# A diffusion trunk step on one core: modulation's column tiles over six stages, other operand places and product order in the w2 groups

## The chip, the core and the metric

The kernel runs on one NeuronCore of a Trainium2 chip. TensorE (PE in the profile; PEld is its weight load) multiplies matrices, VectorE (DVE) and ScalarE (ACT) work on elements, GpSimd (POOL) does almost nothing here, and SyncE (SP) issues the transfers, nearly all on one queue. The metric is the device time of one execution in microseconds. Single runs of this kernel took 1923.6, 1925.41 and 1929.54 us; the median is 1925.41 us.

## The reference, cut to what matters

One layer of a hybrid trunk over 512 latent and 128 context tokens, with D = 1024 features and F = 2816 hidden features, in float32:

```python
def layer(x, mods, l, p, ctx):
    m = [mods[:, j][:, None, :] for j in range(N_MOD)]       # nine modulation vectors
    hh = rmsnorm(x, g[0]) * (1 + m[1]) + m[0]
    x = x + 0.5 * m[2] * swiglu(hh, p['ffn1_w1'][l], p['ffn1_w3'][l], p['ffn1_w2'][l])
    hh = rmsnorm(x, g[1]) * (1 + m[4]) + m[3]
    y, ctx_out = token_mixer(hh, p, l, ctx)                  # differential attention || mLSTM
    x = x + m[5] * y
    hh = rmsnorm(x, g[2]) * (1 + m[7]) + m[6]
    x = x + 0.5 * m[8] * swiglu(hh, p['ffn2_w1'][l], p['ffn2_w3'][l], p['ffn2_w2'][l])
    return x, ctx_out
```

The modulation is `silu(c) @ w_ada + b_ada`, for two vectors (latent and context), 9 x 1024 outputs each. `swiglu(h) = (silu(h @ w1) * (h @ w3)) @ w2`. The token mixer projects to queries, keys, values and gates, runs eight heads of differential attention and four heads of a chunked mLSTM in both directions, and joins the two branches with `w_br_d`, `w_br_m`, `w_out`.

## The kernel before, in words

**Layout.** Features lie on partitions, the 640 tokens along the free dimension, cut in two halves of 320 (`HALF`). The second half holds the last 192 latent and the 128 context tokens, so operations that use a modulation vector are done in two segments there. Each float32 operand is split into a high and a low part (`hH`, `hL`; `wH`, `wL`), and a product is three matmuls (high x high, high x low, low x high).

**The two FFNs** (`HalfStep`) multiply 2 x 2 blocks with seven products in place of eight (Strassen's scheme in Winograd's form). The operands are A11, S1, S2, A12, S3, A22, S4; they are held split, as `hm` parts and `S` tiles. A unit of work is a `Granule`: a raw weight tile, from which `parts` makes the split B and C blocks and `sums` the four summed blocks (`ww`). `products` goes through the list of granules: 20 up granules (w1 and w3 of ten blocks b = 1 to 10; block 0 is done plainly before) and 12 down granules of w2, in three groups q of 3, 4 and 4 blocks with four column granules j each. In each granule the order is A11, S1, the tail A22 of the granule before, S2, A12, the tail S4 of the granule before, S3; A22 and S4 follow as tails in the next granule. Into three PSUM tiles X, Y, Z go the four results; `done(f, hf, ...)` evacuates feature block f of token half hf. The hidden features g are stored to `g_dram` by `store_g` and read back as the operands of the down groups. `at[q, i]` is the place of operand i in group q; `moves` says which operand of the next group is loaded into a place when its last user is done (`used`, in granule j = 3). In group 1 only A11 has a place of its own (`gA`, loaded in `extra`), the others follow one another; in group 2 only A11 takes a place that group 0 has left. `between(i)` is called once per granule, behind the evacuation of A12, and runs the column tiles.

**The modulation.** m0 and m1 are made by TensorE at the start. The other 7 x 1024 outputs are 56 column tiles of 128 (`Columns`): a tile loads 128 x 1024 of `w_ada_c` (`raw_a`, 512 KB), multiplies it with each of the two silu vectors (`csil`) and sums over the row on DVE (line 529, once per vector, each followed by a readout), and adds the bias. Tiles 0 to 12 go with up granules 0 to 12 of the first FFN, two raw buffers; tiles 13 to 23 with its granules 21 to 31, one raw buffer, `csil` read back from `csil_dram` into the place of `SO`; tiles 24 to 55 with heads 0 to 5 of attention, in front of the scores, in the ring of two raw weight buffers. m2 (tiles 0 to 7) is the gate of the first FFN, m3 and m4 (8 to 23) are needed when attention's input is normed, m5 to m8 (24 to 55) from the output projection on.

**Behind the first FFN.** `to_mixing` collects the squares of the new residual (`Stats`), and when the second token half is done, `norm2(0)` takes the root and makes `hH`, `hL` of the first half, which take the places of the `hm` tiles. The rope tables and lambda follow in the code. The first token group does queries and keys of token tiles 0 and 1 together, eight steps over k, with the gate product of the first half in each step and `norm2_second` at k = 1.

**What sets the order.** Matmuls and transposes are kept in program order on TensorE. On the other engines and the SP queue a planner sets the order ahead of time: from what it holds to be ready by its own times, it takes what was traced first. Each engine then runs its list strictly as planned and waits by semaphore, and SP's list of transfers is one of these. An instruction that is ready early can so stand far ahead of its place in the code.

## Time and profile before

| what | value |
|---|---|
| median of three runs | 1925.41 us |
| the profiled execution, its own time | 1932.1 us |
| its span, with the mean granted clock | 1930.3 us, 0.971 |
| busy: PE, DVE, ACT, POOL | 1815.8, 1410.8, 900.2, 4.9 us |
| matmuls | 12490 |
| read from and written to device memory | 246.92 and 77.39 MB |

Times in the rows are microseconds from the span's start unless marked ns. A row of the order of time has start, length, engine, source line, operation, `out<-in` by tile names, partitions x elements, the number merged (x12), and in brackets how long the engine idled before it and what ended that. Line 52 is the matmul helper, line 39 the helper of two-operand DVE work, line 46 scalar operations, line 42 fused ones, line 74 the load helper; so the tile names tell what is done. `raw_a` is a column tile's weight, `p` the softmax weights of a head, `ps_wT` their transposes, `qpk` the packed queries, `nt` the normed input ahead of its shift, `P` the mLSTM's decay matrix. A wait row has engine, line and tile waiting, what it waited for, the total, the times and the longest.

### The profile page before, as it was taken

The page shows a single profiled execution, that of the slowest core. Times are in us where ns is not written, and L with a number is a line of the kernel's source. Part 1 is how long each engine was busy: PE and PEld are TensorE (multiplying, and loading weights), DVE is VectorE, ACT ScalarE, POOL GpSimd, SP SyncE. Part 2 cuts the span into 40 slices and gives each one's busy share as a digit, 9 for nine tenths or more (in the row PEclk, how much of TensorE's full clock was granted, in tenths as well). Part 3 has the DMA queues.
Part 4 walks back from the last instruction along what each step waited for, and adds up shares of the span by engine and source line. Part 5 has one row for each costly group of instructions (what it writes and reads, how often), then busy time and mean ns, then how long its engine had stood idle before and what let it go on. Part 6 is the DMA issues. An engine that isn't in the chain of part 4 may idle for free.

```text
span 1930.3 us, 30868 instructions
## 1 busy us (share of the span) xinstructions
PE 1815.8 (94%) x12490; PEld 1773.5 (92%) x12490; DVE 1410.8 (73%) x2430; ACT 900.2 (47%) x1538; POOL 4.9 (0%) x6
## 2 busy tenths in 40 slices
PE   6898999988797998999999999999999999999999
PEld 4898999888797988989999998899999999999989
DVE  6999887788868685796684544656356888887875
ACT  5644555433444354444454435566234655554432
POOL 1000000000000000000000000000000000000000
PEclk8899999999899999999999999999999999999999
DMA  8366655976415243243232225536434345547972
GB/s 319 128 208 229 224 183 171 389 277 236 170 45 180 97 136 103 88 141 108 85 116 75 90 86 160 162 117 220 167 107 146 115 170 183 176 173 252 372 289 68
DMA packets 142129, 326.32 MB, mean 169 GB/s; under 512 B 10081, under 2 KB 101985, under 8 KB 129313
## 3 DMA queue, kind: packets, MB, share of 16 engines
q1 hardware_dynamic: 141986, 324.34, 48.0%
q8 instruction: 98, 1.61, 0.3%
q14 instruction: 45, 0.37, 0.1%
HBM read 246.92 MB, written 77.39 MB: 168 GB/s over the span
## 4 chain that ended last, share of the span: by engine, by line
PE 76%; DVE 12%; DMA 7%; ACT 3%; issue 2%; SPq 0%; DVEq 0%; ACTq 0%
PE ps_f L52 36%; PE ps_p L52 21%; PE ps_t L52 9%; PE ps_o L52 2%; DMA raw_a<-in_w_ada_c 2%; PE sc L52 2%; PE ps_n L52 2%; DVE raw L39 1%; PE ps_wT L55 1%; DMA hm<-g_dram 1%; PE ps_u L52 1%; DVE raw_a L529 1%; DVE wL L39 1%; PE ps_qkT L55 1%; DMA out_new_c<-Cn 1%
## 5 line engine op out<-in xcount | busy, mean ns | idle before, releaser
L52 PE MATMUL ps_f<-S,ww 128*128 128x320 f32 x2040 | 333.1, 313 | 18.3 <-DVE ww L39 10.4
L52 PEld LDWEIGHTS ps_f<-S,ww 128*128 128x128 f32 x2040 | 310.7, 191 | 20.5 <-DVE ww L39 11.2
L52 PE MATMUL ps_p<-hH,wH 128*128 128x320 f32 x864 | 276.9, 320 | 3.1 <-ACT aT L1186 2.5
L52 PE MATMUL ps_p<-hL,wH 128*128 128x320 f32 x864 | 269.8, 312 | 0.0
L52 PE MATMUL ps_p<-hH,wL 128*128 128x320 f32 x864 | 269.6, 312 | 0.0
L52 PE MATMUL ps_f<-hm,wB 128*128 128x320 f32 x1296 | 212.7, 313 | 11.8 <-DMA hm<-g_dram 11.8
L52 PEld LDWEIGHTS ps_f<-hm,wB 128*128 128x128 f32 x1296 | 198.4, 191 | 12.6 <-DMA hm<-g_dram 12.5
L52 PE MATMUL ps_t<-wH,hH 128*128 128x256 f32 x640 | 187.3, 293 | 6.5 <-ACT hH L201 6.5
L52 PE MATMUL ps_t<-wL,hH 128*128 128x256 f32 x640 | 183.2, 286 | 0.0
L52 PE MATMUL ps_t<-wH,hL 128*128 128x256 f32 x640 | 183.2, 286 | 0.0
L262 ACT ACTIVATE ww<-raw 128x2048 fp32r<-128x2048 f32 (+1 forms) x64 | 119.1, 1861 | 113.0 <-PE ps_f L52 95.5
L52 PEld LDWEIGHTS ps_p<-hH,wH 128*128 128x128 f32 x864 | 165.3, 191 | 4.2 <-ACT aT L1186 2.7
L39 DVE TENSOR_TENSOR ww<-raw,ww 128x2048 fp32r<-128x2048 f32 (+1 forms) x64 | 142.3, 2224 | 34.0 <-ACT ww L262 34.0
L52 PEld LDWEIGHTS ps_p<-hL,wH 128*128 128x128 f32 x864 | 165.3, 191 | 0.5
L52 PEld LDWEIGHTS ps_p<-hH,wL 128*128 128x128 f32 x864 | 164.8, 191 | 0.0
L39 DVE TENSOR_TENSOR raw<-raw 128x512 f32<-128x512 f32 (+3 forms) x192 | 161.2, 841 | 0.3
L52 PE MATMUL ps_f<-hm,ww 128*128 128x320 f32 x840 | 138.0, 313 | 6.4 <-DVE ww L39 6.4
L39 DVE TENSOR_TENSOR wL<-raw,wH 128x2048 fp32r<-128x2048 f32 x49 | 112.1, 2287 | 42.2 <-ACT wH L123 42.2
L123 ACT ACTIVATE wH<-raw 128x2048 fp32r<-128x2048 f32 x49 | 93.7, 1912 | 97.5 <-PE ps_p L52 91.8
L52 PEld LDWEIGHTS ps_f<-hm,ww 128*128 128x128 f32 x840 | 128.4, 191 | 7.7 <-DVE ww L39 7.5
L52 PEld LDWEIGHTS ps_t<-wH,hH 128*128 128x128 f32 x640 | 125.0, 195 | 7.7 <-ACT hH L201 7.4
L52 PEld LDWEIGHTS ps_t<-wL,hH 128*128 128x128 f32 x640 | 124.9, 195 | 0.2
(281 smaller groups left out, 3315.9 us busy)
## 6 DMA issues: line engine op xcount, KB each, us to landing
raw_a<-in_w_ada_c SPq DMA_DIRECT2D x56, 512.0 KB, 3.9
g_dram<-g SPq DMA_DIRECT2D x44, 640.0 KB, 4.4
g_dram<-g SPq DMA_DIRECT2D x44, 480.0 KB, 5.0
hm<-g_dram SPq DMA_DIRECT2D x12, 1280.0 KB, 9.6
S<-g_dram SPq DMA_DIRECT2D x12, 1280.0 KB, 9.4
raw<-in_w1b SPq DMA_DIRECT2D x11, 1024.0 KB, 5.0
raw<-in_w3b SPq DMA_DIRECT2D x11, 1024.0 KB, 4.8
raw<-in_w1a SPq DMA_DIRECT2D x10, 1024.0 KB, 6.1
```

Of the source, the lines that this page charges most:

```text
L39: eng.tensor_tensor(out=out, in0=in0, in1=in1, op=op)
L52: tc.keep_in_program_order(nc.tensor.matmul(*args, **kw))
L55: tc.keep_in_program_order(nc.tensor.transpose(*args, **kw))
L123: act(h, raw, AF.Copy)
L262: act(t[0], flat, AF.Copy)
L529: vec.tensor_tensor_reduce(out=junk, in0=raw, in1=self.csil[:, v, :], op0=ALU.mult, op1=ALU.add, scale=1.0, scalar=0.0, accum_out=mod[:, c ...
```

## The change

1. **Column tiles.** Tiles 0 to 13 go with up granules 4 to 17 of the first FFN. Tiles 14 to 23 go with its granules 21 to 30, each in two halves of 512 of the 1024 inputs (`HalfColumns`): all first halves, then all second halves, two per granule; raw, silu vectors and scratch lie in the place `gB`. Of tiles 24 to 55, twelve stay in attention (behind the scores of query tiles 1 and 3 of heads 0 to 5), eight go with the evacuation of the `w_brd` products, four with that of `w_brm` (their silu vectors are loaded into a tile of their own when the mLSTM stage opens), and the last eight (48 to 55, m8) with up granules 4 to 11 of the second FFN. `between` is called twice per granule, at its start and behind A12's evacuation.
2. **Operand places.** Group 1 gets `gA` and `SO` as fresh places for A11 and S1; the others follow the order (0, 1, 2, 3, 4). Group 2 takes the places of group 0's A22 and S4 for A11 and A12.
3. **Product order.** The tail S4 of the granule before goes ahead of A12. The last granule of the first FFN goes another way (`tokens_early`): A11, A11 x b12 (a product with a further split weight block), the tail A22, A12, S4, the tail S4, S2, S3, S1, A22; so token half 0 is complete with four products to go, at eight products in place of seven.
4. **Behind it.** The rope tables and lambda are queued on DVE behind the last instruction of `norm2(0)`. The first token group of four becomes two of two: queries with the gate product, then keys.
5. **The residual** of the second FFN is read back at granule 16 and not before the granules; its tiles hold the column tiles' data until then.

```diff
-        def parts(self, fp):
+        def parts(self, fp, b12=False):
...
+            E = [(self.two(fp, "C", 512, 3), hi[:, :nk])] if b12 else []
+            for (h, lw), v in [(B, lo), (C, hi[:, nk:]), *E]:
...
                 if not last:
-                    work[i + 1][0].parts(self.fp)
+                    work[i + 1][0].parts(self.fp, tokens_early and i + 2 == n)
+                between(i, 0)
                 X, Y, Z = acc_tile(psum), acc_tile(psum), acc_tile(psum)
                 into(X, A11, True)
                 act(Y, X, AF.Copy)
+                if last and tokens_early:
+                    into(Z, A11, True, "b12")
+                    tail[0]()
+                    into(X, A12, False)
+                    done(0, 0, X, None)
+                    into(Z, A12, False, S4)
+                    done(1, 0, Z, None)
+                    tail[1]()
+                    into(Y, S2, False)
+                    into(Y, S3, False)
+                    u3 = copy_of(Y, "nry")
+                    V = acc_tile(psum)
+                    into(V, S1, True)
+                    done(1, 1, V, u3)
+                    into(Y, A22, False)
+                    done(0, 1, Y, None)
+                    break
...
                 u2 = copy_of(Y, "nacc" if i < 2 * FB - 2 else "nsq", 2)
+                if tail:
+                    tail[1]()
                 into(X, A12, False)
                 done(0, 0, X, None)
-                if tail:
-                    tail[1]()
-                between(i)
+                between(i, 1)
...
-            for q, places in ((1, (None, 0, 1, 2, 3, 4, 5)), (2, ((0, 6), 0, 1, 4, 3, 2, 5))):
+            for q, places in ((1, (None, None, 0, 1, 2, 3, 4)), (2, ((0, 5), 0, 1, (0, 6), 3, 4, 2))):
...
             def extra():
-                at[1, 0] = at[2, 1] = self.fp.tile([128, 2, 4, HALF], F32R, tag="gA", name="op")
-                fetch(1, 0)
+                for i, tag in enumerate(("gA", "SO")):
+                    at[1, i] = at[2, i + 1] = self.fp.tile([128, 2, 4, HALF], F32R, tag=tag, name="op")
+                    fetch(1, i)
                 emptied()
...
+    class HalfColumns:
+        def __init__(self, tiles, csil, junk, raw, then):
+            self.todo = [(h, n) for h in range(2) for n in tiles]
...
+        def tile(self):
...
+            for v in range(2):
+                dot(self.junk, self.raw, self.csil[:, v], to[:, v : v + 1])
+            if h == 0:
+                ts(m, m, b_ada[:, ct : ct + 1], ALU.add)
+            else:
+                tt(vec, m, m, to, ALU.add)
+            self.fetch()
...
-        IN_UP = 13
-        def modulation(i):
-            if i < IN_UP:
...
+        IN_UP = 14
+        def modulation(i, at):
+            if at and 4 <= i < 18:
                 columns.tile()
...
+            elif 20 < i < 31:
+                box["columns"].tile()
...
+    with tc.issue_after(normed2):
+        nc.sync.dma_start(out=cosT, in_=a["cos"])
...
-    tok_group(psum, [(w_q, 0, e_q), (w_k, 0, e_k), (w_q, 1, e_q), (w_k, 1, e_k)], between_first)
+    tok_group(psum, [(w_q, 0, e_q), (w_q, 1, e_q)], between_first)
+    tok_group(psum, [(w_k, 0, e_k), (w_k, 1, e_k)], lambda k: None)
...
-    rest_of = Columns(range(24, 56))
+    order = [*range(24, 32), *range(40, 48), *range(32, 40)]
+    rest_of = Columns(order[:12])
...
-            if hd < 6:
-                for _ in range(2 if qi == 0 and hd in (2, 4) else 1):
-                    rest_of.tile()
             if hd or qi:
                 H.scores(qi)
+            if hd < 6 and qi in (1, 3):
+                rest_of.tile()
...
+    csil2 = ada_p.tile([128, 2, D], F32, name="csil")
+    nc.sync.dma_start(out=csil2, in_=csil_dram.partition_broadcast(128))
+    rest_of = Columns(order[12:])
...
+            if mt == 1:
+                rest_of.tile()
...
+                if (mt, hf) == (1, 1):
+                    rest_of.tile()
...
-    for g in range(4):
-        nc.sync.dma_start(out=x_pairs[g], in_=x2_dram[:, 2 * g : 2 * g + 2, :])
     hs.store_g(hs.SO, 0)
...
+    def modulation2(i, at):
+        if at and 4 <= i < 12:
+            rest.tile()
+        elif at and i == 16:
+            p = pairs("k", "x")
+            for g in range(4):
+                nc.sync.dma_start(out=p[g], in_=x2_dram[:, 2 * g : 2 * g + 2, :])
```

174 lines of the change are left out of this document (105 added, 69 removed).

## The prediction

> **What bounds the kernel now.** I read the page first, then a table of stages, and then each stage's gaps in the order of time.
>
> ```profile
> span 1930.3 us, 30868 instructions
> PE 1815.8 (94%) x12490; PEld 1773.5 (92%) x12490; DVE 1410.8 (73%) x2430; ACT 900.2 (47%) x1538; POOL 4.9 (0%) x6
> ```
>
> TensorE (PE) is busy 94% of the span, so no change that leaves its products alone can win more than the 114.5 us in which it idles, plus what it loses at a lowered clock. The question is which stages hold those losses. The next table has, for each stretch, its length, each engine's busy time with its instructions, the granted clock and the DMA share.
>
> ```profile
> core 0: us, PE busy (x) PEld busy (x) DVE busy (x) ACT busy (x) POOL busy (x), PEclk, DMA share, GB/s
> 78.00:190.00 112.00, 100.67 (x655) 99.62 (x655) 110.39 (x166) 54.53 (x74) 0.00 (x0) 0.95 0.67 233
> 190.00:337.00 147.00, 147.00 (x1004) 147.00 (x1003) 119.97 (x156) 78.21 (x108) 0.00 (x0) 1.00 0.56 196
> 337.00:501.00 164.00, 146.54 (x952) 144.22 (x950) 138.79 (x235) 61.39 (x87) 0.00 (x0) 0.96 0.77 283
> 501.00:522.00 21.00, 9.01 (x40) 7.19 (x41) 17.12 (x41) 9.04 (x16) 0.00 (x0) 0.67 0.77 272
> 586.00:1020.00 434.00, 406.03 (x3064) 397.05 (x3064) 319.41 (x550) 191.08 (x366) 0.00 (x0) 0.96 0.35 114
> 1020.00:1150.00 130.00, 129.29 (x973) 127.40 (x972) 66.00 (x111) 54.56 (x109) 0.00 (x0) 1.00 0.26 87
> 1318.00:1440.00 122.00, 121.32 (x830) 121.03 (x829) 58.28 (x102) 47.80 (x62) 0.00 (x0) 1.00 0.47 168
> 1518.00:1763.00 245.00, 245.00 (x1659) 244.67 (x1660) 204.66 (x263) 132.50 (x182) 0.00 (x0) 0.99 0.51 179
> 1763.00:1931.00 168.00, 156.21 (x1030) 154.76 (x1028) 117.33 (x183) 60.24 (x82) 0.00 (x0) 0.97 0.69 254
> ```
>
> The rows are: first FFN's up granules while column tiles run; the same without them; its down granules; its end; attention heads 0 to 5 (with column tiles); heads 6 and 7 (without); the branch products; the second FFN's up and its down granules. Two stretches without columns (190 to 337, 1518 to 1763) have no PE idle at all; their twins with columns lose time. From 190 to 337 a matmul takes 147/1004 = 0.1464 us, so a product of 12 is 1.76 us and an up granule of 84 is 12.3 us, and VectorE (DVE) is free for 27.0 us in 12.0 granules, 2.26 us each.
>
> **Columns in the first FFN's up granules.** A column tile is two dot products and an addition.
>
> ```profile
> L529 DVE CUSTOM_DVE_ANT_0 junk<-raw_a,csil x26: 1212/1219/1224, 90.7 to 178.0; 128x1024 bf16<-128x1024 f32 x26
> 586.00:1020.00 434.00, 78.56 (x128) 0.96 0.35 114
> 177.69 3.03 PE L52 MATMUL ps_f<-S,ww 128*128 128x320 f32 x10 [4.62 <-DVE ww L39]
> ```
>
> The second row is line 529 alone in attention: 78.56 us for 64 dot products with their readouts, so 2.46 us a tile, 2.6 with the addition. The 13 tiles, in the code one per granule 0 to 12, ran between 90.7 and 178 us, that is in 7.2 granules: 33.8 us of work against 16.3 us free, 17.5 too much. PE lost 112 - 655 x 0.1464 = 16.1 us there, in stalls as that at 177.69. The loss is DVE's excess. The change puts 14 tiles (36.4 us) into granules 4 to 17. If they stay one per granule, 31.6 us are free and 4.8 are lost; if the planner again draws them together into 7.7 granules, 36.4 - 17.4 = 19.0 are lost. They now stand behind the splits of granules 0 to 4, but the old ones ran early although the code had them later, so I take 12: -4 us (-11 to +3).
>
> **The first FFN's down granules.** Three things change. The operand places: q=1 gets two fresh places instead of one and q=2 inherits two that are free early, so that in each handover five transfers instead of six hang on the last products of the group before. The tail S4 moves ahead of A12. And 11 column tiles become 10, each cut into two halves with its own fetch.
>
> ```profile
> 453.00 3.57 PE L52 MATMUL ps_f<-hm,wB 128*128 128x320 f32 x12 [7.71 <-DMA hm<-g_dram]
> DVE csil L529 <- DMA raw_a<-in_w_ada_c: 4.7, 2, 4.3
> 433.91 1.23 DVE L529 CUSTOM_DVE_ANT_0 csil<-raw_a,csil 128x1024 bf16<-128x1024 f32 x1 [4.33 <-DMA raw_a<-in_w_ada_c]
> hm<-g_dram SPq DMA_DIRECT2D x12, 1280.0 KB, 9.6
> 511.29 0.23 DVE L977 CUSTOM_DVE_ANT_0 tab<-tab 128x64 f32<-128x64 f32 x1 [1.55 <-DMA tab<-in_lam]
> ```
>
> The q=1 to q=2 handover stalls 7.71 us on A12, then runs twelve matmuls in 3.57 us. Before, A12 of q=2 took the place of S3, the fifth product of q=1's last granule; it was wanted five products later, 8.8 us, less than the 9.6 us a transfer takes. After, it takes a place that q=0 left. That stall goes. But DVE is nearly full here: 138.8 us busy, against 952 x 0.1464 = 139.4 us of products. The halves cost it more. From 64 columns in 0.23 us and 1024 in 1.22, 512 take 0.69; a half tile is 1.66 us with readouts (0.08 each) and 0.13 of addition, 20 of them 33 us against 11 x 2.6 = 28.6. Its 25 us of idle time include the waits for PE that go with the stall and for fetches that will be more frequent. I take 0: what the operands give, DVE takes back. Bounds: -17 (stage loss of 24.6 with the stall, its slow clock and the DVE stalls gone, the 6 at the start staying) to +20 (one us of wait in each half).
>
> **The end of that FFN.** The last granule does A11·b12 in addition (one product, 1.76 us), so token half 0 finishes four products ahead of the end, and the rope tables queue behind the norm.
>
> ```profile
> 499.05 1.92 PE L52 MATMUL ps_f<-S,ww 128*128 128x320 f32 x12
> 507.26 1.43 PE L52 MATMUL ps_ss<-nsq,ones 128*128 128x320 f32 x2 [4.25 <-ACT nsq L181]
> 509.26 0.49 DVE L48 TENSOR_SCALAR rv<-ps_ss 128x320 f32<-128x320 f32 x1
> 514.00 1.01 DVE L42 SCALAR_TENSOR_TENSOR nt<-x,scale,ry 128x320 f32<-128x320 f32 x2
> 515.21 0.58 PE L52 MATMUL ps_t<-wH,hH 128*128 128x256 f32 x1 [6.51 <-ACT hH L201]
> ```
>
> Products end at 499.05 + 12 x 0.1464 = 500.8; the first of attention begins at 515.21, 14.4 us later. Only the sum of squares (2.0 us, 507.26 to 509.26), the root (4.74 us to 514.00, of which the lam wait 1.55 above and some 0.8 of table work go) and the first column (1.2) must follow: 5.6, say 6.2 us. That gives 8.2, less 1.76: -6 us, the split of b12 (0.7 us of DVE by the row of 64 and 1024) lying a granule earlier (-9, to +1.8 if the statistics are late again). The statistics' own matmul stays behind the last product in PE's order. Splitting the first token group changes no instruction; 6 + 3 matmuls per column stand against DVE's 1.06 us per column (514.00 and its twin take 2.1 per pair), with the k products behind. No cost; if DVE lags it is on the path, inside the +1.8.
>
> **Attention.** 32 column tiles become 12, behind the scores.
>
> ```profile
> 622.29 1.54 PE L55 MATMUL ps_wT<-ident,p 128*128 128x128 f32 x6 [4.48 <-DVE p L42]
> 593.48 1.23 DVE L529 CUSTOM_DVE_ANT_0 raw_a<-raw_a,csil 128x1024 bf16<-128x1024 f32 x1 [3.48 <-DMA csil<-csil_dram]
> DVE raw_a L529 <- DMA raw_a<-in_w_ada_c: 30.3, 20, 3.8
> 590.05 1.32 PE L55 MATMUL ps_qkT<-identr,qpk 128*128 128x128 f32 x10 [4.02 <-DVE qpk L39]
> 761.48 1.54 PE L55 MATMUL ps_wT<-ident,p 128*128 128x128 f32 x6 [2.65 <-DVE p L42]
> 1136.43 0.82 PE L55 MATMUL ps_wT<-ident,p 128*128 128x128 f32 x6
> ```
>
> PE idles 28.0 us in heads 0 to 5 and 0.7 in heads 6 and 7. All but the gap at 590 (rope work, 4.0) end on the softmax chain p, and DVE meanwhile waited 30.3 us, 20 times, for column fetches: each such wait holds everything queued on DVE. That is 24 us of gaps; the clock, 0.96 over 434 us against 1.00 later, is worth up to 17, of which I count half, since part falls into the gaps. Of 32 us, 12/32 stay: -20 us (-32, to 0 if the remaining tiles sit on the same chains).
>
> The clock shows at 761.48: six transposes took 1.54 us behind a 2.65 us gap, 0.82 with none. [...]
>
> **Where the columns go.** Twelve tiles, 31 us, go to the branch products, where DVE is idle 63.7 of 122 us: covered. They share two weight buffers, though: +1 (0 to +5). The new silu vectors load ahead of the mLSTM's first transfers:
>
> ```profile
> 1170.42 0.91 PE L52 MATMUL ps_n<-va,P 128*128 128x258 f32 x2 [2.26 <-issue]
> 1166.88 0.82 DVE L39 TENSOR_TENSOR P<-P,mask 128x640 f32<-128x640 f32 x1 [8.30 <-DMA P<-nm_dram]
> ```
>
> 1 MB at the 389 GB/s of the page's fullest slices is 2.6 us on the chain that ends at 1170.42: +2.5 (0 if issued early, +4.3 with a slow clock). Eight tiles go into the second FFN's up granules 4 to 11: 20.8 us against 8 free shares of (245 - 204.66)/19.9 = 2.03, 16.2. Spread, 4.6 lost; drawn together as in the first FFN, 16.1/13 x 8 = 9.9; over all 20 granules, nothing. I take +4 (0 to +9.9). The residual's reload moves from before the granules to granule 16: three granules, 37 us, cover its 2.6 MB (some 7 us at that rate); without them the first down granule would wait those 7.
>
> **The second FFN's down granules** have no columns.
>
> ```profile
> 1878.32 3.57 PE L52 MATMUL ps_f<-hm,wB 128*128 128x320 f32 x12 [4.08 <-DMA hm<-g_dram]
> GB/s 319 128 208 229 224 183 171 389 277 236 170 45 180 97 136 103 88 141 108 85 116 75 90 86 160 162 117 220 167 107 146 115 170 183 176 173 252 372 289 68
> ```
>
> The same handover: 4.08 us, and 3.57 for twelve and a slow product after it. DVE has room (117 of 168). I take -6 (-6.8 to 0).
>
> **Sum**: -4 + 0 - 6 - 20 + 1 + 2.5 + 4 - 6 = -28.5. The profiled execution took 1932.1 us, 6.7 above the median of the three runs; 1903.6 against it is 1897 against the median of 1925.4.
>
> **Rivals.**
> *DVE gives little back.* Tiles are drawn together again in both FFNs (+7 and +6 against my terms) and 8 of attention's 20 fail to come: 1918. For it: 13 tiles ran in 7.2 granules. Against: heads 6 and 7 without columns. Chance 0.2.
>
> *All of it comes.* The up granules lose only 4.8, the handover goes without a price from DVE, attention keeps the rope gap alone: -11 - 12 - 8 - 30 - 6.5, and +4 elsewhere, 1862. For it: stretches without columns lose nothing. Against: DVE's 138.8 us beside 139.4 of products. 0.15.
>
> *Half tiles block DVE: slower.* A half is fetched only when the one before is done, into one buffer, through the queue that carries the operands:
>
> ```profile
> raw<-in_w2a SPq DMA_DIRECT2D x8, 384.0 KB, 9.6
> raw_a<-in_w_ada_c SPq DMA_DIRECT2D x56, 512.0 KB, 3.9
> ```
>
> Between two halves DVE has some 5.0 us of other work (12.3 - 2.26 in a granule, halved). If a half lands after 3.9 us it never waits; if after 9.6, as weight pieces do in this very stage, each of 20 waits 4.6 us, 92 in all, 67 beyond the 25 that DVE idles: 1964. It decides the sign from a wait of (28.5 + 25)/20 = 2.7 us a half, a landing of 7.7 us. For it: 4.33 us at 433.91. Against: only two of eleven fetches were waited for. 0.08. [...]
>
> *It does not do what it says.* What runs when follows from the planner's readiness, not from the place in the code; with reloads, tables and tiles where they were, 1925. 0.05.
>
> **How the numbers follow.** The forecast of 1897 holds 0.52; its own range is 1880 to 1912. The bounds' distances, added as squares, are about 23 us down and 31 up; eight times in ten they reach 1875 to 1924, and the range is widened to 1868 to 1925 for a part of the second rival, so that most of it and the slower one stay outside. A change of 0.3%, 5.8 us, is about what a measurement of this kernel can tell from none. Faster: 0.52 + 0.15 + 0.13 of the first rival, 0.80; same: 0.05 and 0.05 of it, 0.10; slower 0.10.
>
> **What would show it.** Right: between the FFN's end and attention the gap falls from 14.4 to about 6 us, with no lam wait ahead of the norm; no PE gap on an operand at q=1 to q=2 in either FFN; in heads 0 to 5 PE idle near 14 us, fetch waits under a third of 30.3; in the up granules columns spread over ten or more granules. Wrong: DVE waits for raw_a in the first FFN's down granules beyond 25 us; PE waits for sums (ww) in the second FFN's granules beyond 5 us; a gap above 5 us at the mLSTM's first product; weights late in the branch products. The forecast falls if attention's gaps stay though its tiles are gone.

## The result, and the profile after

The changed kernel takes 1950.3 us (median of four runs, 1949.1 to 1950.8) against 1926.4 us before: a ratio of 1.0123, 95% interval 1.0105 to 1.0140. It is slower by 1.2%, where 1897 us were forecast.

The page of the changed kernel, its span and the busy time of its engines:

```profile
span 1948.3 us, 30989 instructions
PE 1811.4 (93%) x12502; PEld 1768.4 (91%) x12502; DVE 1419.9 (73%) x2480; ACT 899.1 (46%) x1537; POOL 4.9 (0%) x6
```

TensorE has twelve matmuls more than before, those of A11·b12, and every one is in the trace (12490 before, 12502 after). So the two executions can be laid side by side by count: a stage of the kernel after begins where as many matmuls have started as at that stage's first microsecond before (from the first FFN's end on, twelve more). This is the table of stretches of the changed kernel, cut at those places, in the columns of the prediction's table; the seventh row, the mLSTM, was not shown of before.

```profile
77.30:191.10 113.80, 100.78 (x654) 99.31 (x653) 109.75 (x169) 53.04 (x73) 0.00 (x0) 0.96 0.67 233
191.10:340.30 149.20, 147.28 (x1005) 147.02 (x1004) 123.83 (x158) 78.30 (x109) 0.00 (x0) 1.00 0.57 197
340.30:503.30 163.00, 148.67 (x964) 145.69 (x962) 133.22 (x250) 61.24 (x86) 0.00 (x0) 0.96 0.74 269
503.30:544.70 41.40, 8.44 (x42) 7.13 (x41) 24.05 (x60) 8.89 (x16) 0.00 (x0) 0.59 0.55 174
609.00:1015.80 406.80, 394.58 (x3064) 387.74 (x3065) 271.52 (x448) 189.73 (x366) 0.00 (x0) 0.99 0.29 95
1015.80:1145.70 129.90, 129.20 (x973) 127.30 (x972) 65.92 (x111) 54.58 (x109) 0.00 (x0) 1.00 0.26 87
1145.70:1318.50 172.80, 163.54 (x945) 150.43 (x945) 100.03 (x316) 98.27 (x244) 0.00 (x0) 0.96 0.47 150
1318.50:1449.60 131.10, 122.87 (x829) 122.34 (x828) 84.48 (x157) 47.72 (x62) 0.00 (x0) 0.97 0.56 201
1527.70:1780.00 252.30, 245.49 (x1659) 244.70 (x1660) 224.89 (x305) 131.58 (x182) 0.00 (x0) 0.99 0.56 195
1780.00:1948.30 168.30, 156.40 (x1031) 154.88 (x1029) 119.07 (x182) 59.45 (x82) 0.00 (x0) 0.97 0.69 254
```

Heads 0 to 5 of attention need 406.8 us for the 3064 matmuls that took 434.0; that is the large gain, and it came in full. But from 503.3 to 544.7 TensorE does in 41.4 us what it did in 21.0, and the branch products (131.1 against 122.0) and the second FFN's up granules (252.3 against 245.0) are longer too. The stages' differences, at equal counts, beside the terms of the prediction, in us:

| stage (its limits in the profile before) | predicted | measured |
|---|---|---|
| start to 78 | 0 | -0.7 |
| first FFN, up granules (78 to 337) | -4 | +4.0 |
| its down granules (337 to 500) | 0 | -2.6 |
| its end, to the first token groups (500 to 522) | -6 | +22.0 |
| the rest of the first products, heads 0 to 7 (522 to 1150) | -20 | -27.0 |
| mLSTM (1150 to 1318) | +2.5 | +4.8 |
| branch products, output projection (1318 to 1518) | +1 | +9.2 |
| second FFN, up granules (1518 to 1763) | +4 | +7.3 |
| its down granules, to the end | -6 | +1.0 |
| sum | -28.5 | +18.0 |

The limits can be read to some 0.3 us. The sum is the difference of the two spans, 1948.3 and 1930.3. The medians differ by 23.8: the profiled execution of before took 5.7 us more than the median, that of after no more than its own. What makes these 5.8 us the stages of one execution can't tell.

The largest miss is at the first FFN's end. In order of time, the changed kernel's last product, the statistics' root, the half tiles (line 559) and attention's first product:

```profile
501.53 1.92 PE L52 MATMUL ps_f<-S,ww 128*128 128x320 f32 x12
...
511.56 0.49 DVE L42 SCALAR_TENSOR_TENSOR ry<-rt,ry 128x320 f32<-128x320 f32 x1
515.17 0.69 DVE L559 CUSTOM_DVE_ANT_0 raw_a<-raw_a 128x512 bf16<-128x512 f32 x1 [3.12 <-DMA raw_a<-in_w_ada_c]
...
519.99 0.69 DVE L559 CUSTOM_DVE_ANT_0 raw_a<-raw_a 128x512 bf16<-128x512 f32 x1 [3.19 <-DMA raw_a<-in_w_ada_c]
...
533.88 0.69 DVE L559 CUSTOM_DVE_ANT_0 raw_a<-raw_a 128x512 bf16<-128x512 f32 x1 [2.90 <-DMA raw_a<-in_w_ada_c]
...
535.55 0.17 DVE L42 SCALAR_TENSOR_TENSOR scale<-mod,g_norm 128x16 f32<-128x16 f32 x1
...
537.16 0.58 PE L52 MATMUL ps_t<-wH,hH 128*128 128x256 f32 x1 [32.49 <-ACT hH L201]
```

The products end at 503.3 and the root is there at 512.05. The norm lacks only its scale, which needs the last of the half tiles, and they come one by one: fetch, two dot products, sum, next fetch. From 515.17 to 533.88 are four steps, 4.7 us each, of which VectorE waits about 3.1. Scale is made at 535.55, and attention's first product starts at 537.16: 33.9 us behind the last product, where it was 14.4 before. Here is the view of that tile in this stretch (start of the first and of the last dot product, VectorE's waits, time from issue to landing), first before, with the row in which scale is made, and then after:

```profile
L529 DVE CUSTOM_DVE_ANT_0 csil<-raw_a,csil x22: 1214/1220/1227, 378.1 to 497.3; 128x1024 bf16<-128x1024 f32 x22
500.28 0.17 DVE L42 SCALAR_TENSOR_TENSOR scale<-mod,g_norm 128x16 f32<-128x16 f32 x1
```

```profile
L559 DVE CUSTOM_DVE_ANT_0 raw_a<-raw_a x40: 678/690/694, 384.3 to 534.6; 128x512 bf16<-128x512 f32 x40
...
  DMA raw_a<-in_w_ada_c: 23.8, 12
...
DMA to landing us min/median/max: 2.9/3.2/9.8
```

Before, the last dot product began at 497.3, 3.5 us ahead of the last product's end at 500.8. Scale was there at 500.45 and was first used at 514.00 (`nt<-x,scale,ry`, in the prediction's rows), when the root was ready: the chain had 13.5 us to spare. After, the root is there at 512.05 and scale at 535.72: the change used up the time to spare, and scale is 23.7 us late.

Other waits, from the wait lists of six stretches of the changed kernel (first FFN's up granules 77 to 191, attention, mLSTM, branch products with two rows, second FFN's up granules, its down granules with two rows):

```profile
PE ps_f L52 <- DVE ww L39: 10.1, 3, 4.5
...
DVE raw_a L559 <- DMA raw_a<-in_w_ada_c: 10.5, 9, 2.3
...
PE ps_n L52 <- DVE P L39: 4.2, 1, 4.2
...
DVE raw_a L559 <- DMA raw_a<-in_w_ada_c: 15.5, 6, 3.8
...
PE ps_p L52 <- DVE y L39: 7.2, 1, 7.2
...
PE ps_f L52 <- DVE ww L39: 6.8, 3, 2.6
...
PE ps_f L52 <- ACT ww L264: 3.4, 1, 3.4
...
PE ps_f L52 <- DVE ww L39: 1.8, 1, 1.8
```

In attention VectorE now waits 10.5 us for columns instead of 30.3. In the branch products it waits 15.5 us for them, six times, and once TensorE stands 7.2 us for an evacuation (y). The chain of work that ends this stall, in order of time:

```profile
1380.32 1.13 DVE raw_a L559
1381.48 4.76 DMA raw<-in_w_brm
1386.34 1.92 ACT wH L123
1388.28 2.14 DVE wL L39
1390.49 0.89 DVE y L39 x2
1391.52 0.60 PE ps_p L52
```

The evacuation stands in VectorE's list behind the split (wL) of a weight tile. That tile's load was issued at 1381.48 only, when a column tile had left the ring of weight buffers that both share. In both FFNs' up granules TensorE waits for the sums of the weights (ww): in the first for 10.1 us, as before the change (10.4), and 2.9 more on ScalarE's part; in the second for 6.8, where it waited for none. In the second FFN's down granules it waits no longer for the operand hm (4.1 us before) but for those sums, first on ScalarE's part of them and then on VectorE's (the last two rows).

### The profile page after: what moved, and what is told of

Its sections match the earlier page's. It is cut to its first block, busy times and chain, and to the rows that moved or that the text cites. A ratio compares the mean times of both kernels' runs of the same rounds, so it can differ in the third digit from the quotient of the medians.

```text
span 1948.3 us, 30989 instructions
## 1 busy us (share of the span) xinstructions
PE 1811.4 (93%) x12502; PEld 1768.4 (91%) x12502; DVE 1419.9 (73%) x2480; ACT 899.1 (46%) x1537; POOL 4.9 (0%) x6
## 4 chain that ended last, share of the span: by engine, by line
PE 68%; DVE 14%; DMA 9%; ACT 3%; issue 3%; SPq 0%; DVEq 0%; ACTq 0%
PE ps_f L52 29%; PE ps_p L52 17%; PE ps_t L52 11%; DMA raw_a<-in_w_ada_c 5%; PE sc L52 2%; PE ps_o L52 2%; DVE raw_a L559 2%; PE ps_n L52 2%; DVE raw L39 1%; DVE ww L39 1%; DMA S<-g_dram 1%; PE ps_wT L55 1%; PE ps_u L52 1%; DVE wB L39 1%; DVE junk L559 1%
## 5 line engine op out<-in xcount | busy, mean ns | idle before, releaser
L52 PE MATMUL ps_f<-S,ww 128*128 128x320 f32 x1944 | 318.7, 312 | 28.3 <-DVE ww L39 18.8
L52 PEld LDWEIGHTS ps_f<-S,ww 128*128 128x128 f32 x1944 | 295.4, 190 | 31.7 <-DVE ww L39 20.8
L52 PE MATMUL ps_t<-wH,hH 128*128 128x256 f32 x640 | 186.0, 291 | 32.5 <-ACT hH L201 32.5
L52 PEld LDWEIGHTS ps_p<-hH,wH 128*128 128x128 f32 x864 | 164.3, 190 | 10.9 <-issue 7.4
L52 PEld LDWEIGHTS ps_t<-wH,hL 128*128 128x128 f32 x640 | 123.4, 193 | 0.8 <-DVE hL L42 0.8
L52 PE MATMUL ps_f<-hm,ww 128*128 128x320 f32 x744 | 121.8, 315 | 0.0
## 6 DMA issues: line engine op xcount, KB each, us to landing
S<-g_dram SPq DMA_DIRECT2D x10, 1280.0 KB, 10.9
```

Source lines behind the costliest of these rows:

```text
L52: tc.keep_in_program_order(nc.tensor.matmul(*args, **kw))
```

## The experiments

All ratios are to the kernel before, run beside each, with 95% intervals. Stage differences are at equal counts, against the one profile before; since that execution took 5.7 us more than its median, two runs compare better with each other than either with it.

### The half tiles behind the last product

Run e5: the second halves are left out.

```diff
-            self.todo = [(h, n) for h in range(2) for n in tiles]
+            self.todo = [(h, n) for h in range(1) for n in tiles]
```

> The changed kernel without the second halves of tiles 14 to 23 (that part of the modulation is left out: ten half tiles in place of twenty). Theory A (the half tiles that run behind the last product hold the norm's scale, and so attention's start): the tenth half ended near 466 in the changed kernel, so nothing is left behind the last product; the first product of attention falls from 537.2 to about 513, total 1926 (1922 to 1930). Theory B (attention's start waits for something else, the statistics, the residual's store or the weights of v): it stays above 525 and the total above 1938.

Measured: 1924.1 us, 0.9979 (0.9965 to 0.9993), 26.2 us less than the changed kernel. The first FFN's end in its order of time:

```profile
503.67 1.92 PE L52 MATMUL ps_f<-S,ww 128*128 128x320 f32 x12
...
513.64 0.58 PE L52 MATMUL ps_t<-wH,hH 128*128 128x256 f32 x1 [6.98 <-ACT hH L201]
```

Attention starts 8.2 us behind the last product (505.4 to 513.64), and that end is 4.0 us shorter than before in place of 22.0 longer. Theory A holds: nearly all of the 26.2 us come from the half tiles that ran behind the last product.

Run e9 leaves nothing out. It takes four more tiles into the up granules, each queued on VectorE behind the last instruction traced before it (`lately[0]`), and so halves only six.

```diff
-        IN_UP = 14
+        IN_UP = 18
...
-            if at and 4 <= i < 18:
-                columns.tile()
+            if at and i < 18:
+                with tc.issue_after(lately[0]):
+                    columns.tile()
```

> The changed kernel with 18 tiles in the first FFN's up granules 0 to 17, each queued on VectorE behind the work traced before it, and so only six tiles (12 halves) in its down granules; nothing is left out. Theory A (the chain of halves sets attention's start): ten halves were done by 466 and 12 need some 15 us more, so all end before the last product; the gap between the last product and attention falls from some 33 to 8 or 9 us, and the up granules win about 10: total 1917 (1910 to 1923). Rival (halves as such, whatever their number, block VectorE): the gap stays above 20 and the total above 1928.

Measured: 1924.9 us, 0.9985 (0.9972 to 0.9998); 8 us slower than expected, but the end did what theory A says:

```profile
L565 DVE CUSTOM_DVE_ANT_0 raw_a<-raw_a x24: 678/684/694, 379.6 to 483.8; 128x512 bf16<-128x512 f32 x24
...
501.96 0.70 PE L58 MATMUL ps_ss<-nsq,ones 128*128 128x320 f32 x2
510.00 0.58 PE L58 MATMUL ps_t<-wH,hH 128*128 128x256 f32 x1 [7.33 <-ACT hH L207]
```

The last half begins at 483.8, ahead of the products' end at 501.4, and attention starts 8.6 us behind that end. The eight us are missing in the first FFN's up granules, which won 3 of the 10 us hoped for (+1.0 against before, +4.0 in the changed kernel), and in the second FFN's (+13.6, where the changed kernel lost 7.3 with the same code).

Runs e1 and e2 were to tell a chain with one buffer from the work of the halves. In e1 three raw buffers:

```diff
-            nc.sync.dma_start(out=self.raw, in_=a["w_ada_c"][gi, :, i, ks])
+            nc.sync.dma_start(out=self.raw[self.asked % len(self.raw)], in_=a["w_ada_c"][gi, :, i, 512 * h : 512 * h + 512])
...
+            whole = fp.tile([128, 2 * D], F32, tag="s4", name="csil").rearrange("p (v k) -> p v k", v=2)
```

> The changed kernel, but the half tiles 14 to 23 get three raw buffers in place of one (the whole silu vectors lie in a place that is free, so they aren't reloaded); same 20 halves, same DVE work (33 us), same places in the code. Theory A, the serial chain (fetch, half tile, fetch, about 4.7 us each) that stands behind the last product sets the start of attention: the first product of attention falls from 537.2 to about 514 us, total 1927 (1922 to 1932). Theory B, the DVE work of the halves and their place in DVE's list set it, whatever the buffers: first product of attention still after 530, total 1944 to 1952.

In e2 ten whole tiles with one buffer, the silu vectors in the same place s4:

```diff
-            elif 20 < i < 31:
+            elif at and 20 < i < 31:
                 box["columns"].tile()
...
+            csil = fp.tile([128, 2 * D], F32, tag="s4", name="csil").rearrange("p (v k) -> p v k", v=2)
...
+            c = Columns(range(IN_UP, 24))
```

> The changed kernel, but tiles 14 to 23 are whole tiles again, one per granule 21 to 30, with one raw buffer (the scheme of the kernel before, in other places); DVE work 26 us in place of 33. Theory A (serial chain of 20 short fetches): ten fetches with a longer tile behind each, at most 6.5 us each, fit into the 120 us of the stage: first product of attention near 513, total 1925 (1920 to 1930), equal to the kernel with three buffers within 4 us. Theory C (what costs is DVE's 7 us of work more for halves): gain of 7 us or less, 1943 or more.

Measured: e1 1935.4 us, 1.0038 (1.0021 to 1.0055); e2 1944.3 us, 1.0085 (1.0061 to 1.0109). In e1 neither theory's number came; in e2 that of theory C did (1943 or more), but it doesn't bear that theory out, because in both the place wasn't free: s4 holds the operand S3. The views of the silu vectors and of the half tiles in e1:

```profile
L762 SPq DMA_DIRECT2D csil<-csil_dram x2: 344/384/424, 456.1 to 456.5; - x2
...
L559 DVE CUSTOM_DVE_ANT_0 raw_a<-raw_a,csil x40: 678/686/694, 462.9 to 526.0; 128x512 bf16<-128x512 f32 x40
```

The vectors could be loaded at 456.1 only, when the operand had left, and the first half ran at 462.9. So the totals don't settle what the buffers are worth. The trace of e1 does show what they do to a step: VectorE waited for halves twice, 2.6 us in all, in place of 12 times and 23.8 us, and behind the last product a half that was fetched ahead followed the one before in 1.7 us (518.39 and 520.05) in place of 4.7. The 20 halves took 63 us (462.9 to 526.0, 3.2 us each), and attention began 2.5 us behind the last dot product's start, at 528.56. The same 2.5 to 2.9 us stand between the start of the last dot product and attention's first product in every run in which the tiles came late: 534.6 and 537.2 (changed kernel), 531.9 and 534.8 (e2), 531.5 and 534.1 (e4), 521.7 and 524.2 (e6), 536.6 and 539.1 (e8), wherever the products had ended.

### Attention and what follows, alone

Run e3 is the kernel before with only the columns behind the first FFN moved.

```diff
-    rest_of = Columns(range(24, 56))
+    order = [*range(24, 32), *range(40, 48), *range(32, 40)]
+    rest_of = Columns(order[:12])
...
+            if hd < 6 and qi in (1, 3):
+                rest_of.tile()
...
+    rest = Columns(range(48, 56))
```

> The kernel before, with only the columns of attention and later moved (12 in attention behind the scores, 12 with the branch products, 8 in the second FFN's up granules, residual reloaded at granule 16); both FFNs' products, operand places and the first FFN's columns stay as before. Theory: the stages are independent, so attention gives what it gave in the changed kernel (-27 between the products of 522 and 1150), mLSTM costs 5, branch products 9, second FFN's up granules 7, the end 3: total 1924 (1919 to 1929). Rival: attention's -27 came in part from the split token group or from tables queued behind the norm: attention gives only 15 to 20 and the total is 1932 to 1937.

Measured: 1927.8 us, 0.9996 (0.9983 to 1.0009): no difference. By stages: attention -25.4, mLSTM +2.3, branch products +8.5, the second FFN's up granules +11.7. The theory's stages hold but for the last, which lost nearly five more than thought, and the split token group has little part in attention's gain. The columns had not become cheaper, they had moved: what attention won, the three stages behind it gave back nearly whole.

### Spreading the tiles

Run e6 is the changed kernel with three edits; e7 has them on e3.

```diff
+                with tc.issue_after(lately[0]):
                     columns.tile()
...
+        r = mp.tile([128, 2, T], F32, tag="so", name="raw_a").rearrange("p a b -> p (a b)")[:, :D]
+        nc.sync.dma_start(out=r, in_=src)
...
-        if at and 4 <= i < 12:
-            rest.tile()
+        if at and i % 2 == 1 and i < 16:
+            with tc.issue_after(lately[0]):
+                rest.tile()
```

> The changed kernel with three edits, each read in its own stage. (1) In the first FFN's up granules each column tile is queued on VectorE behind the last VectorE work traced before it, so the planner can't draw them together: theory, drawn-together tiles cost what was lost there, the up granules get 11 to 14 us faster; rival, VectorE's total work or transfers cost it, nothing. (2) The branch products' tiles get a raw place of their own, eight of them, and four more go to attention: theory, the shared raw weight buffers cost the 9 us, branch products 8 to 9 us faster and attention 2 to 4 slower; rival, VectorE's work costs it, 3 us or less. (3) The second FFN's eight tiles spread over its up granules 1 to 15, queued likewise: theory, its up granules 7 us faster; rival, nothing. Total by the theories 1926 (1920 to 1932), by the rivals 1945 or more.

> The kernel before with the columns of attention and later moved as in the run of the middle alone (1927.8), and the same three edits: columns of the first FFN's up granules queued in place (13, granules 0 to 12), eight branch tiles with a raw place of their own and 16 in attention, the second FFN's eight tiles spread. First FFN's products, operand places and end as in the kernel before. By the theories: up granules -13, branch -6 net of attention, second FFN -11: 1898 (1892 to 1906). By the rivals 1920 or more.

Measured: e6 1932.6 us, 1.0016 (1.0000 to 1.0032); e7 1915.5 us, 0.9922 (0.9896 to 0.9948). The totals are 7 and 17 above the theories', but the edits separate by stage. Two rows of e6's table of stretches, the part of the up granules that was full of columns and the second FFN's up granules:

```profile
77.40:174.30 96.90, 96.35 (x655) 95.83 (x655) 85.77 (x115) 53.48 (x74) 0.00 (x0) 1.00 0.62 219
...
1516.50:1763.30 246.80, 246.44 (x1660) 245.61 (x1660) 223.76 (x303) 127.14 (x182) 0.00 (x0) 0.99 0.60 197
```

The 655 matmuls that took 112.0 us before and 113.8 after take 96.9 here; over all up granules it is -6.8 in place of +4.0 (-10.1 in e7, with 13 tiles). Between these two kernels the planner's drawing together was the loss. The second FFN's up granules lose 1.8 in place of 7.3, with the same eight tiles. Edit 2 failed: the branch products, now with eight tiles in one buffer of their own, still lose 7.0 and 6.2, and the four tiles that went to attention cost it 4 to 5 us. The first FFN's end stays 22.6 longer in e6: its products end 14 us earlier than in the changed kernel, and attention starts only 13 earlier, behind the last half.

### What the branch products lose

Run e13 leaves the twelve tiles of that stage out.

```diff
-    rest_of = Columns(order[12:])
...
+    rest_of = Columns([])
+    for n in order[12:]:
+        vec.tensor_copy(mod[:, 16 + n, :], b_ada[:, 16 + n, None].to_broadcast([128, 1, 2])[:, 0])
...
```

> The changed kernel without the twelve tiles of the branch products (their products are left out, those modulation values are the bias alone); the silu vectors are still loaded when the mLSTM opens. Theory F, the tiles cost the branch stage its loss, through their place in VectorE's list and in the raw ring: from the first branch product to the output projection 8 to 9 us are won, the mLSTM's loss stays, total 1941. Rival, the loss is not the tiles' (late reloads of z and the gates): 3 us or less, 1947 or more.

Measured: 1940.5 us, 1.0083 (1.0065 to 1.0101). The stage in the table of stretches:

```profile
1317.00:1439.00 122.00, 121.33 (x830) 121.03 (x829) 58.35 (x102) 47.95 (x62) 0.00 (x0) 1.00 0.47 169
```

122.0 us, as before the change: theory F holds, the tiles are the whole loss. A place of their own doesn't take it away: eight tiles still cost 6.2 us (e7), 0.8 each, as twelve do in the shared ring. The way is another one. With the ring the weights came late behind the tiles, as the chain above shows; in e7 VectorE waits for the tile's own fetch, and TensorE for an evacuation behind it:

```profile
PE ps_p L58 <- DVE y L41: 5.3, 1, 5.3
...
DVE junk L535 <- DMA raw_a<-in_w_ada_c: 18.7, 7, 4.4
```

So VectorE, busy for 58.35 of 122.0 us without the tiles, was no cover for tiles whose transfers came late (18.7 us of waits in e7) ahead of an evacuation in its list. How much of the loss in the changed kernel is the list and how much the late weights was not separated.

### The w2 groups: order and places

Run e4 takes the old order with the new places, e8 the new order with the old places.

```diff
                 into(X, A12, False)
                 done(0, 0, X, None)
+                if tail:
+                    tail[1]()
                 between(i, 1)
```

> The changed kernel, but the tail S4 goes behind A12 again in both FFNs. Theory D: the stalls of the sums (4.8 us near 416, 5.1 us near 1866) come from the order, which puts the splits of the next weights behind one more evacuation on ACT and DVE: both go, 4 to 8 us are won, 1943 to 1946, and between 1763 and the end the second FFN is 5 us ahead of the changed kernel. Rival: the raw weights land late there, whatever the order: nothing won, or the operand stalls come back (+4 to +8), 1950 to 1958.

```diff
-            for q, places in ((1, (None, None, 0, 1, 2, 3, 4)), (2, ((0, 5), 0, 1, (0, 6), 3, 4, 2))):
+            for q, places in ((1, (None, 0, 1, 2, 3, 4, 5)), (2, ((0, 6), 0, 1, 4, 3, 2, 5))):
...
-                for i, tag in enumerate(("gA", "SO")):
+                for i, tag in enumerate(("gA",)):
```

> The changed kernel with the operand places of the kernel before in both FFNs (group 1 has one fresh place, group 2 takes one from group 0), all else as changed. Theory E, the places removed the operand stalls (7.7 and 4.1 us) and the stalls of the sums (4.8 near 416, 5.1 near 1866) came with them, in their place: sums' stalls go, operand stalls return, total 1950 within 4. Rival, the two are apart: the operand stalls return on top, 1956 to 1963.

Measured: e4 1950.4 us, 1.0112 (1.0093 to 1.0132), no difference to the changed kernel, so theory D fails; e8 1948.4 us, 1.0094 (1.0068 to 1.0119). The totals hide it, since e8 loses 6.6 us more at the first FFN's end and 5.5 more in the second FFN's up granules. In the second FFN's down granules, where no columns run, the four combinations stand so, against before: old order and old places 0 (e3 within 0.4 of it), old order and new places +1.8 (e4), new order and new places +1.0 (changed kernel), new order and old places -5.6 (e8). Other runs with the same two settings spread: new order and new places -1.8 to +1.5 (e1, e2, e5, e6, e9, e13), new order and old places -3.5 to -4.9 (e10 to e12). The two ranges don't meet. TensorE's waits in that stage in e8 and, as the last row, its wait for the operand in the first FFN's down granules:

```profile
PE ps_f L52 <- ACT wC L249: 2.0, 1, 2.0
PE ps_f L52 <- DMA S<-g_dram: 1.3, 1, 1.3
PE ps_f L52 <- DMA hm<-g_dram: 1.0, 1, 1.0
...
PE ps_f L52 <- DMA hm<-g_dram: 6.0, 4, 4.2
```

In the second FFN the order alone takes the operand stall from 4.1 to 1.0 us and brings no stall of the sums. With the new places the operand stall is gone or small (none in the changed kernel, 0.8 in e4), and the sums come late in its place: 5.1 us in the changed kernel (3.4 on ScalarE, 1.8 on VectorE), 4.6 in e4. In the first FFN the down granules are 6.8 shorter than before in e8, 2.6 in the changed kernel. Theory E is right that the sums' stalls came with the places: in the first FFN, too, the waits for sums are 4.3 us in e8 and 10.9 in the changed kernel. That the operand stalls would return was right in the first FFN (6.0 us, 7.7 before) and wrong in the second. Why the new places make the sums late was not found: the weights' load there is issued just behind the sums of the granule before, in both.

### Compositions

Runs e10, e11 and e12 put the findings together: new order, old places, the last token half early, whole column tiles in the first FFN's down granules as before (which the old places make room for), tiles queued in place in both FFNs' up granules.

```diff
+            t = fp.tile([128, 2560], F32, tag="SO", name="csil")
...
+            raw = fp.tile([128, D], F32, tag="gB", name="raw_a")
+            c = Columns(range(IN_UP, 24))
...
-            if at and 4 <= i < 18:
-                columns.tile()
+            if at and i < 14:
+                with tc.issue_after(lately[0]):
+                    columns.tile()
```

> A composition: the changed product order (S4 ahead of A12, token half 0 early), operand places as before, the first FFN's down columns as whole tiles as before (10), 14 tiles queued in place in up granules 0 to 13, the second FFN's eight spread over its up granules, 16 tiles in attention, and in the branch products six with a raw place of their own (every second unit) and two in the weight ring. By the stages of the runs so far: 1915 of the composition on the kernel before, less 5 each for the two FFNs' down granules by the order, 4 for the early tokens and 4 for the branch: 1897 (1890 to 1905). If the order's gain needs the half tiles' timing, 1905 to 1912.

> The same composition, but attention's twelve tiles and the branch products' twelve in the shared raw ring as in the changed kernel. If the cost of the branch products is the shared ring, its branch products lose 9 against the kernel before and those with own places 3 or less, attention being 4 faster: total 2 above the other composition, 1899. If it is that VectorE's list has an evacuation behind a tile whose transfer is late, both lose the same there and this one is the faster by 4: 1893.

> The composition with the branch tiles in the shared ring (1904.6), its 14 tiles of the first FFN's up granules moved from granules 0 to 13 to granules 4 to 17, queued in place as before. If where they are spread counts (in the run of the changed kernel spread, with granules 4 to 17, the up granules ended 7.4 us ahead of the kernel before, with 0 to 13 only 2 to 3): 5 us won, 1900 (1896 to 1903). If that difference came from elsewhere: 1903 to 1907.

Measured: e10 1908.7 us, 0.9909 (0.9883 to 0.9934); e11 1904.6 us, 0.9885 (0.9866 to 0.9904); e12 1904.5 us, 0.9894 (0.9876 to 0.9911). All three are faster than both kernels, and e10 and e11 lie 12 us above the better case of their expectations (1897 and 1893); e11 is 45.7 us below the changed one by the medians. Its page:

```profile
span 1901.4 us, 30908 instructions
PE 1806.3 (95%) x12502; PEld 1763.6 (93%) x12502; DVE 1414.0 (74%) x2430; ACT 891.7 (47%) x1537; POOL 4.9 (0%) x6
```

Against before its stages are: up granules -1.5, down -3.2, end -4.3, attention -26.5, mLSTM +1.9, branch +7.5, second FFN -2.6 (+1.1 and -3.7). e10's place of its own for six branch tiles wins 1.3 there and its four tiles more in attention cost 5.6, so e11's second bet has the relation right and the level wrong: both lose about the same in the branch, and e11 is the faster by 4. In e12 the up granules won 3.6 more than in e11, and the down granules gave 4.3 back: the total is the same.

e10's total is in the range of its second case, but not for that case's reason: the order's gain came without half tiles, -3.2 to -3.8 in the down granules of each FFN in e10 and e11. What fell short are the up granules. The compositions counted on some -10 there, as in e7; -2.1 (e10), -1.4 (e11) and -5.1 (e12) came, and with 18 tiles +1.0 (e9), although the tiles are spread in all of them. TensorE's waits for VectorE's sums there fell from 12.0 us in the changed kernel to 3.1 (e12), 4.2 (e6) and 6.7 (e10, e11). Why the same spread gives so little in some places was not found.

## Why the prediction was wrong, point by point

**The end of the first FFN** (-6, measured +22.0) is the step that failed; it is 28 of the 46.5 us between forecast and profile. "Only the sum of squares", the root "and the first column (1.2) must follow", the text said. It counted what follows in the norm's own chain and put at nothing, without a reason, that the norm's scale also waits for tile 23. Before, scale was made 13.5 us ahead of its use; in the changed kernel six halves came behind the last product, and scale was 23.7 us late. The term itself, without the tiles, is -4.0 to -4.3 (e5, e9, e11), near the -6 and inside its bounds: attention starts 8.2 to 8.6 us behind the last product, not 6.2.

**The rival that came**, half tiles, was there with 0.08. Its mechanism was named rightly: "A half is fetched only when the one before is done, into one buffer". Its place was wrong. It added up VectorE's waits within the stage and let the sign turn at 2.7 us a half; the 12 waits were 2.0 us each, 23.8 in all, just under the 25 us that were named as the mark. What decides is not the sum of the waits but where the chain ends: 20 halves from 384.3 to 535.5, 7.6 us each, where the time from 384.3 to the products' end, 119.0 us, left 5.95 for each. Only 14 began in that time, 8.5 us each, though VectorE waited just 7.3 us for them there; the six behind the last product have the other 16.5 us of waits. What set the pace inside the stage, VectorE's planned list or the landings, was not separated. From 515.17 to 533.88, behind the last product, VectorE had no other work to cover its waits of 2.9 to 3.2 us each.

**First FFN, up granules** (-4, measured +4.0). The right mechanism was picked as an alternative: 14 tiles drawn together into 7.4 granules (89.8 to 180.2), as early as the 13 before (90.7 to 178.0) though the code has them four granules later. The result lies just outside the bound of +3. The text took a middle of 12 us between 4.8 and 19.0 although the trace had shown the upper case for 13 tiles; e6 shows that it is the drawing together (-6.8 without). The sign missed by choosing between two cases instead of weighing how the planner had treated the same loop.

**Its down granules** (0, measured -2.6): right, and for the reason given, that the handover stall goes and other stalls take the gain. What took it was the sums (ww): TensorE waited 10.9 us for them (6.1 on VectorE, 4.8 on ScalarE), 5.8 before. Whether the halves' work on VectorE makes them late was not separated; in the second FFN's down granules, which have no halves, they are late as well.

**Attention** (-20, measured -27.0; -25.4 alone in e3): right in mechanism, with the clock's part mis-sized. PE idles 12.2 us in heads 0 to 5 (406.80 - 394.58) where the text said 14, so the gaps gave 15.8 us, as forecast; VectorE's waits for columns are 10.5 us, where it asked for under a third of 30.3. The rest came from the matmuls themselves: the same 3064 were busy 406.0 us before and 394.6 after, 11.5 less, where some 5 had been counted (20/32 of half of 17). One gap that the text put down to the softmax chain, 2.4 us at 598.5, ended on kpk.

The clock shows in the trace of before at the prediction's own row at 761.48: behind a gap of 2.65 us six transposes are slow (1.54 us, 0.82 elsewhere), and the granted clock there is 1.00 from 755 to 761.1, 0.50 from 761.2 to 764.5 and 1.00 again from 765 to 767. Over heads 0 to 5 it rose from 0.96 to 0.99 with the gaps gone, as the rows had said; and behind the 32.5 us gap at 537 the products were slow at first. In the order of time, the last slow product of attention and one behind it with a quarter more columns:

```profile
541.11 0.41 PE L52 MATMUL ps_t<-wL,hH 128*128 128x256 f32 x1
...
541.48 0.31 PE L52 MATMUL ps_g<-hH,wgH 128*128 128x320 f32 x1
```

The granted clock is 0.50 from 537.16 to 541.40 and 1.00 from there to 544.70: it is back some 4.2 us behind the start, with short gaps in between.

**mLSTM** (+2.5, measured +4.8, and 1.8 to 4.2 in the other runs): right in kind; the wait for P before its first product is 4.2 us where it was 2.3.

**Branch products** (+1, 0 to +5; measured +9.2) failed. The text called the tiles "covered" because DVE was idle 63.7 of 122 us, and priced the shared buffers at +1. e13 shows that the tiles are all of the loss. The chain of the 7.2 us stall shows late weights behind a column tile in the shared ring, which the text had named as a sign of being wrong; e7 shows as much loss per tile without the ring. Two steps fail: the size of the shared buffers' term, and taking an engine's idle share as cover. In that chain y stood behind a split in VectorE's list: TensorE's products had ended at 1384.3, VectorE idled 2.2 us for the split, and y ran at 1390.49 only.

**Second FFN, up granules** (+4, measured +7.3, and 6.9 to 13.6 elsewhere with the same code): the case "drawn together", 9.9, was the upper bound, and five of the other runs lie above it. The eight tiles ran from 1547.8 to 1616.8, in 5.6 granules. The mechanism is shown by e6 and the compositions, where the spread tiles cost 1.0 to 1.8 (2.8 in e7).

**Second FFN, down granules** (-6, measured +1.0) failed. The operand stall went as said, but it was taken to leave nothing in its place, and a stall of the sums of 5.1 us was next. The order without the places does give -5.6 (e8) and -3.5 to -4.9 (e10 to e12): the change contained the gain and lost it by its other half.

## What to carry to other kernels

When work is moved along a serial chain of fetch, compute, fetch with one buffer, work out when its last link ends and who needs it first, not how long each link waits; the trace before shows how much time it has to spare (here 13.5 us from scale to its use), and the six links left behind the last product took 32 us. Before idle time of an engine is taken as cover for more work, look whether the data is there when that work's turn comes in its list: VectorE's 63.7 idle us of 122 didn't cover twelve tiles for whose transfers it waited 15.5 us, and the stage grew by 9.2. Spreading work over a loop meant fixing its place in that list, as the order in the code did not (96.9 us in e6 where the changed kernel took 113.8). An edit made of two parts that aim at one stall should be tried in all four combinations: here, in the second FFN's down granules, one part alone won 3.5 to 5.6 us and both together next to nothing.

## What the runs showed of the hardware

A transfer of half the size landed 0.6 us sooner by the medians. The half tiles' 256 KB took a median of 3.2 us from issue to landing in the changed kernel, the 512 KB of whole tiles 3.8 us in e2, in the same stage:

```profile
DMA to landing us min/median/max: 3.6/3.8/10.5
```

Other runs of the same stage have longer medians, and they are again close: 6.2 us for e9's halves, 6.6 for the whole tiles before. By the first two medians two halves in a chain wait 6.4 us where a whole tile waits 3.8, an estimate.
